# A hybrid RWKV-7, RG-LRU, attention and ConvFFN block on one Trainium2 core: smaller first loads with fifteen constant products, and the output's last row made by token halves

## The chip, the cores and the metric

The kernel runs on one core of one Trainium2 chip. The metric is the device time of one execution in microseconds (us). The kernel before was timed in three runs: 895.38, 891.78 and 893.97 us, median 893.97 us.

## The reference

One layer of a streaming encoder on `x` (1 x 512 tokens x 1024 channels, float32) with a fixed memory `mem` of 256 rows. Every sub-layer begins with an RMS norm. Cut to what matters:

```
h   = rms_norm(x, norm_mix)
p   = h @ W_in + b_in                        # 38 blocks of 128 columns
x  += merge(rwkv7(p[RWKV]), rglru(p[B]))     # two recurrent branches, gated and projected
m   = rms_norm(mem, norm_mem)
k,v = split(m @ W_kv)                        # 1024 columns each
x  += softmax(q k^T / 16) v @ W_o            # q = rms_norm(x) @ W_q, 4 heads
u   = rms_norm(x) @ W_in_ffn                 # 2 x 2816 columns
x  += (gelu(causal_dwconv(u_gate)) * u_up) @ W_out
out = rms_norm(x, norm_fin)
```

Two places are touched by the change: the beginning, where `k` and `v` are made from the memory and `h` from `x`, and the end, where the last product with `W_out` is added to `x`, and the final norm scales the output.

## The kernel before, in words

Everything lies transposed: channels on the 128 partitions, tokens in the columns. A float32 product is made of three products of the type fp32r: each operand is split into a high part (ScalarE rounds it) and a low part (VectorE subtracts the high part from the value), and `mm3` (L165) issues high by high (L166), high by low (L167) and low by high (L168) into one PSUM bank. So each block of 128 weight rows by 128 output rows costs three loads of 128x128 weights and three products over the columns.

Weights are streamed in blocks of 128 x 1024 (512 KB) by SyncE's queue, through four raw buffers, and three buffers each for the high (`wh`) and low (`wl`) part. `stream` (L100) issues the load (L106), the cast on ScalarE (L117) and the remainder on VectorE (L118); the first two blocks are cast in halves of 512 columns. A cast into `wh` waits until TensorE has read the block three back. A scheduler puts the instructions of the program in order on each engine: what stands in `tc.high_priority()` goes as early as it can, `tc.issue_after(x)` puts an instruction behind `x` on its engine, and `keep_in_program_order` keeps the written order.

**The beginning.** TensorE issues `NWAKE` = 11 products of a constant (`wake`, L288), which need no data. The memory `mT` comes in two halves of 512 KB (`load_m`, L296), with the first block of `wk` between them. `split_m(k)` (L304) scales one eighth of the memory by the norm weights `gm` on ScalarE (L306) into the high part and on VectorE (L307) into the low part. Splits 0 to 2 and 3 stand ahead of the casts of the first `wk` block (`fill` with a lambda, L315), the rest behind. Then K is made in eight blocks `m` of 24 products of 256 columns each (`k_ps`), in four banks, two blocks to a bank. The memory's own norm is applied behind the product: squares (`m_squares`, after block 2), their sums `rs_ps` and `rmc_ps` on TensorE (`m_norm`, after block `KNORM` = 5), and then each block is scaled by `rm` into a buffer `kt` (L348, six buffers) and stored to `dK` by GpSimd's queue (L349). V follows: two column halves of 512, for each two banks `v_ps` and 48 products of 512 columns (L166 to L168, with `wv` as the moving side), with the casts of `wv` in the same `wh` and `wl` buffers. `x_norm` (L377) makes `hT`, the normed `x`, in eight parts on VectorE and ScalarE (L382 to L384); the first products with `W_in` (`in_ps`) follow. Small constants for the branches (`dp`, L409 to L452) are made on VectorE after the last block of K.

**The end.** `W_out` is applied in seven groups of products, `out_product` (L1347) for each; the last is `s4`, which adds into the right half of the four banks `YZ` (256 tokens, `oyz_ps`), 4 rows `m` of 11 blocks, 33 products of 256 columns for a row. After each row `c12` (L1422) is called: VectorE adds the bank to `x` (`xr`, L1380), ScalarE squares it (L1382), and for the last row, `m` = 3, this is done for two token halves of 128, and `final` (L1391) follows for each half: the sum of squares over channels on TensorE with a matrix of ones (plain float32, L1394 and L1395), Ln and two Exp on ScalarE (L1406 to L1408), the scaling of all eight channel blocks on GpSimd and VectorE (L1411), and three stores, one by ScalarE's queue (L1415) and two by SyncE's (L1413).

## Time and profile before

| | |
|---|---|
| median of 3 runs | 893.97 us (891.78 to 895.38) |
| profiled execution | 894.56 us, span 892.8 us, mean granted clock 0.996 |
| TensorE busy (PE) | 877.4 us, 98% of the span, 6197 instructions |
| VectorE busy (DVE) | 685.2 us, 77% |
| ScalarE busy (ACT) | 513.6 us, 58% |
| GpSimd busy (POOL) | 132.5 us, 15% |
| DMA | 201.37 MB, mean 226 GB/s |

The profile is of one execution: the span runs from its first to its last recorded event, and all times of rows are in us from its start. PE rows are products, PEld rows are the loads of their weights, which overlap with products. Products are pipelined: a row's own duration (0.28 us for 256 columns) is longer than the distance to the next one, so the price of a product in a stream is the distance from start to start. A row marked "xN" joins N instructions that follow each other on the engine; its duration is from the first to the last. What stands in brackets is the idle time ahead of it and the instruction that ended it. ACTq and SPq rows are issues of DMAs by those engines. The granted clock is TensorE's, as a share of its full 2.4 GHz.

### The profile page before, as it was taken

To read this page: it belongs to the slowest core of one execution; us is meant where nothing else is said; L and a number is where in the kernel's file an instruction comes from. 1 tells how busy PE (TensorE), PEld (TensorE's weight loads), DVE (VectorE), ACT (ScalarE), POOL (GpSimd) and SP (SyncE) were. 2 spreads that over 40 slices of the span, in tenths; PEclk is the share of its full clock that TensorE was granted. 3 is DMA by queue.
4 is the path that set the end of the run, shared out by engine and by line. 5 is a ranking of instruction groups with operands and counts; after the bars stand their busy time and mean duration, and the time that the engine had idled before them with its cause. 6 is when DMAs were issued, how large, how long until landed. Compare 5 with 4: busy or idle time off the path is not lost.

```text
span 892.8 us, 15934 instructions
## 1 busy us (share of the span) xinstructions
PE 877.4 (98%) x6197; PEld 767.9 (86%) x6197; DVE 685.2 (77%) x1104; ACT 513.6 (58%) x783; POOL 132.5 (15%) x163
## 2 busy tenths in 40 slices
PE   8999999999999999999999999999999999999996
PEld 7878878888877677888888778999999999999996
DVE  6796598777967677675575578889888889999674
ACT  6575676634347676233554466766655656757563
POOL 0101222021102021001122111111111111211100
PEclk9999999999999999999999999999999999999999
DMA  7878899678997279758888958999999999998963
GB/s 268 307 253 215 206 228 233 187 203 233 262 227 156 72 203 249 220 166 229 218 234 183 197 137 185 260 275 271 265 255 294 263 297 275 244 276 220 261 202 94
DMA packets 97242, 201.37 MB, mean 226 GB/s; under 512 B 19536, under 2 KB 30928, under 8 KB 97104
## 3 DMA queue, kind: packets, MB, share of 16 engines
q1 hardware_dynamic: 62240, 118.57, 40.4%
q0 software_dynamic: 25504, 67.38, 36.9%
q10 hardware_dynamic: 9424, 14.42, 4.7%
q8 instruction: 48, 0.79, 0.4%
q14 instruction: 26, 0.21, 0.1%
HBM read 188.54 MB, written 78.12 MB: 299 GB/s over the span
## 4 chain that ended last, share of the span: by engine, by line
PE 91%; DVE 4%; DMA 2%; ACT 1%; issue 1%; DVEq 0%; ACTq 0%; SPq 0%
PE in_ps L167 7%; PE in_ps L166 7%; PE in_ps L168 7%; PE fx_ps L167 5%; PE fx_ps L166 5%; PE fx_ps L168 5%; PE fyz_ps L167 4%; PE fyz_ps L166 4%; PE fyz_ps L168 3%; PE ox_ps L166 2%; PE oyz_ps L166 2%; PE ox_ps L168 2%; PE oyz_ps L168 2%; PE oyz_ps L167 2%; PE ox_ps L167 2%; PE co_ps L167 2%
## 5 line engine op out<-in xcount | busy, mean ns | idle before, releaser
L132 ACT CAST wfi_h<-wfi_r 128x1024 fp32r<-128x1024 f32 x77 | 81.1, 1053 | 71.5 <-PE fx_ps L167 19.7
L168 PE MATMUL in_ps<-hT,win_l 128*128 128x512 f32 x304 | 121.3, 399 | 0.0
L167 PE MATMUL in_ps<-hT,win_h 128*128 128x512 f32 x304 | 121.0, 398 | 0.2 <-DVE hT L384 0.2
L166 PE MATMUL in_ps<-hT,win_h 128*128 128x512 f32 x304 | 120.6, 398 | 0.3 <-DVE pr L586 0.3
L133 DVE TENSOR_TENSOR wfi_l<-wfi_r,wfi_h 128x1024 fp32r<-128x1024 f32 x77 | 94.1, 1222 | 22.7 <-ACT wfi_h L132 22.4
L482 POOL DMA_DIRECT2D dS<-in_wfi x66 | 66.7, 1028 | 293.1 <-PE in_ps L166 102.3
L167 PEld LDWEIGHTS in_ps<-hT,win_h 128*128 128x128 f32 x304 | 57.1, 188 | 14.2 <-issue 0.7
L166 PEld LDWEIGHTS in_ps<-hT,win_h 128*128 128x128 f32 x304 | 57.1, 188 | 13.2 <-DVE pr L586 0.7
L168 PEld LDWEIGHTS in_ps<-hT,win_l 128*128 128x128 f32 x304 | 57.1, 188 | 13.1 <-issue 0.7
L518 POOL DMA_DIRECT2D dOs<-in_wfo x54 | 39.8, 784 | 181.5 <-PE fyz_ps L166 54.0
L118 DVE TENSOR_TENSOR win_l<-win_r,win_h 128x1024 fp32r<-128x1024 f32 x38 | 46.3, 1221 | 24.2 <-ACT win_h L117 20.7
L117 ACT CAST win_h<-win_r 128x1024 fp32r<-128x1024 f32 x38 | 39.9, 1050 | 41.1 <-PE in_ps L167 32.4
L1341 DVE TENSOR_TENSOR wfo_l<-wfo_r,wfo_h 128x1024 fp32r<-128x1024 f32 (+1 forms) x39 | 47.2, 1209 | 15.2 <-ACT wfo_h L1340 15.2
L1340 ACT CAST wfo_h<-wfo_r 128x1024 fp32r<-128x1024 f32 (+1 forms) x39 | 40.5, 1039 | 31.3 <-DMA wfo_r<-dOs 11.6
L168 PE MATMUL ox_ps<-go,wfo_l 128*128 128x256 f32 x176 | 49.1, 279 | 0.8 <-DVE wfo_l L1341 0.8
L166 PE MATMUL ox_ps<-go,wfo_h 128*128 128x256 f32 x176 | 49.2, 279 | 0.4 <-ACT wfo_h L1340 0.3
L166 PE MATMUL fx_ps<-hq,wfi_h 128*128 128x256 f32 x176 | 49.4, 280 | 0.0
L166 PE MATMUL fyz_ps<-hq,wfi_h 128*128 128x256 f32 x176 | 49.2, 280 | 0.0
L167 PE MATMUL fx_ps<-hq,wfi_h 128*128 128x256 f32 x176 | 49.2, 280 | 0.0
L167 PE MATMUL fyz_ps<-hq,wfi_h 128*128 128x256 f32 x176 | 49.2, 280 | 0.0
L167 PE MATMUL fx_ps<-hr,wfi_h 128*128 128x256 f32 x176 | 49.2, 280 | 0.0
L166 PE MATMUL fx_ps<-hr,wfi_h 128*128 128x256 f32 x176 | 49.2, 279 | 0.0
(432 smaller groups left out, 2704.9 us busy)
## 6 DMA issues: line engine op xcount, KB each, us to landing
dS<-in_wfi POOLq DMA_DIRECT2D x66, 512.0 KB, 7.8
wfi_r<-dS SPq DMA_DIRECT2D x44, 512.0 KB, 6.8
win_r<-in_win SPq DMA_DIRECT2D x38, 512.0 KB, 5.3
wfi_r<-in_wfi SPq DMA_DIRECT2D x33, 512.0 KB, 5.8
dS<-dS POOLq DMA_DIRECT2D x22, 512.0 KB, 5.7
dOs<-in_wfo POOLq DMA_DIRECT2D x12, 512.0 KB, 7.9
wk_r<-in_wk SPq DMA_DIRECT2D x8, 512.0 KB, 5.1
wv_r<-in_wv SPq DMA_DIRECT2D x8, 512.0 KB, 4.0
```

The lines of the kernel that those rows point to most:

```text
L117: casts.append(S.copy(hi[:, o:o + n], raw[:, o:o + n]))
L118: V.tensor_tensor(lo[:, o:o + n], raw[:, o:o + n], hi[:, o:o + n].bitcast(F32), ALU.subtract)
L132: S.copy(hi, raw)
L133: V.tensor_tensor(lo, raw, hi.bitcast(F32), ALU.subtract)
L166: first = PE.matmul(ps, lh, rh, start=start, stop=False, **kw)
L167: PE.matmul(ps, lh, rl, start=False, stop=False, **kw)
L168: PE.matmul(ps, ll, rh, start=False, stop=stop, **kw)
L482: return lambda: nc.gpsimd.dma_start(s(out), src, **kw)
L518: yield lambda k=k, w=w, src=src: nc.gpsimd.dma_start(dO[n, m][:, k * P:(k + w) * P], src, **kw)
L1340: S.copy(hi[:, :n], raw[:, :n])
L1341: V.tensor_tensor(lo[:, :n], raw[:, :n], hi[:, :n].bitcast(F32), ALU.subtract)
```

## The change

At the beginning: fifteen constant products instead of eleven; the memory's first half comes as two quarters, with the first block of `wk` between them and the second half behind; the splits of the first quarter (two) stand ahead of the first cast and the other six behind it; the squares come after block 1 and the norm after block 4; eight `kt` buffers; and the `dp` operations from the Exp on stand behind the last `hT`. At the end: `out_product` of `s4` makes its last row in two passes of 33 products of 128 columns, one for each token half, keeping the eleven weight blocks; the add and square of the first half are issued after the first pass, its `final` behind the sixth block of the second pass, and the second half's add, square and `final` after that pass.

```diff
--- before.py
+++ after.py
@@ -32,8 +32,8 @@
 IN_REST = [22, 23, 24, 25, 26, 27, 28, 29, 30, 31, 32, 33, 34, 35, 36, 37, 14, 15, 16, 17, 18, 19, 20, 21]
 NEARLY = 3
 NMID = 10
-NWAKE = 11
-KNORM = 5
+NWAKE = 15
+KNORM = 4
 NPOOL = 2
 KVB = 3
 IN_ORDER = IN_RWKV + IN_REST
@@ -293,12 +293,11 @@
         mraw = p0.tile([P, KB, NMEM], F32, name="mraw")
         xraw = p0.tile([P, KB, T], F32, name="xraw")
 
-        def load_m(q):
+        def load_m(k, e):
             with tc.high_priority():
-                mdma.append(tc.keep_in_program_order(
-                    nc.sync.dma_start(mraw[:, 4 * q:4 * q + 4, :], mT_d[:, 4 * q:4 * q + 4, :])))
-
-        load_m(0)
+                mdma.append(tc.keep_in_program_order(nc.sync.dma_start(mraw[:, k:e, :], mT_d[:, k:e, :])))
+
+        load_m(0, 2)
         m2 = p0.tile([P, 2, KB, NMEM], F32R, name="m2")
 
         def split_m(k):
@@ -309,15 +308,15 @@
             return hi
 
         with tc.high_priority():
-            for k in range(3):
+            for k in range(2):
                 split_m(k)
         un = Units(wk_d, "wk")
-        un.fill(lambda i: load_m(1) if i == 0 else split_m(3))
+        un.fill(lambda i: [load_m(2, 4), load_m(4, KB)] if i == 0 else None)
         tc.keep_in_program_order(nc.scalar.dma_start(pv, pv_d))
         mss = p0.tile([P, NMEM], F32, name="mss")
         msq = [p0.tile([P, NMEM], F32, tag="msq", name=f"msq{k}", bufs=2) for k in range(KB)]
         with tc.high_priority():
-            for k in range(4, KB):
+            for k in range(2, KB):
                 last_m = split_m(k)
         def m_squares():
             with tc.issue_after(casts[-1].ins):
@@ -344,7 +343,7 @@
         last_k = None
 
         def k_out(m):
-            kt = p0.tile([P, NMEM], F32, tag="kt", name=f"kt{m}", bufs=6)
+            kt = p0.tile([P, NMEM], F32, tag="kt", name=f"kt{m}", bufs=8)
             ins = V.tensor_tensor(kt, k_ps[m], rm, ALU.mult)
             nc.gpsimd.dma_start(dK[m], kt)
             return ins
@@ -357,7 +356,7 @@
             if m >= 4:
                 with tc.issue_after(wdma[-1].ins):
                     nc.sync.dma_start(xraw[:, 2 * m - 8:2 * m - 6, :], xT_d[:, 2 * m - 8:2 * m - 6, :])
-            if m == 2:
+            if m == 1:
                 m_squares()
             if m == KNORM:
                 m_norm()
@@ -381,7 +380,8 @@
                 hf32 = p0.tile([P, T], F32, tag="hf32", name=f"hf32_{k}", bufs=2)
                 V.scalar_tensor_tensor(hf32, xraw[:, k, :], par("nmix", k), rx, ALU.mult, ALU.mult)
                 S.copy(h2[:, 0, k, :], hf32)
-                V.tensor_tensor(h2[:, 1, k, :], hf32, h2[:, 0, k, :].bitcast(F32), ALU.subtract)
+                last_h = V.tensor_tensor(h2[:, 1, k, :], hf32, h2[:, 0, k, :].bitcast(F32), ALU.subtract)
+            return last_h
 
         st = stream(wv_d, "wv")
         for hf in range(2):
@@ -395,7 +395,7 @@
                         sl = slice(i * P, (i + 1) * P)
                         mm3(pss[i], m2[:, 0, kb, sl], m2[:, 1, kb, sl], rh, rl, kb == 0, kb == KB - 1)
             if hf == 0:
-                x_norm()
+                last_h = x_norm()
             for i in range(2):
                 vt = p0.tile([P, T], F32, tag="vt", name=f"vt{hf}_{i}", bufs=2)
                 S.activation(vt, pss[i], AF.Copy, scale=rmc[:, i:i + 1])
@@ -435,6 +435,7 @@
             V.tensor_scalar(la, lam, -1.0, None, ALU.mult)
             V.tensor_tensor(la, la, lam, ALU.min)
             S.activation(le, la, AF.Exp)
+        with tc.issue_after(last_h.ins):
             V.tensor_scalar(la, le, 2.0, None, ALU.add)
             V.reciprocal(la, la)
             V.tensor_tensor(lz, le, la, ALU.mult)
@@ -1344,9 +1345,9 @@
 
     uf = out_weights()
 
-    def out_product(n, i, out, start, done, nsum=0):
-
-        for m, k in out_order:
+    def out_product(n, i, out, start, done, nsum=0, halves=False):
+
+        for m, k in out_order[:-HB] if halves else out_order:
             wh, wl = next(uf)
             g = gsets[i][k // 8][:, k % 8]
             ins = mm3(out[m], wh, wl, g[:, 0, :], g[:, 1, :], start and k == 0, k == HB - 1,
@@ -1355,6 +1356,19 @@
                 sum_behind(ins)
             if k == HB - 1:
                 done(m)
+        if halves:
+
+            w = [next(uf) for _ in range(HB)]
+            for o in (0, P):
+                for k, (wh, wl) in enumerate(w):
+                    g = gsets[i][k // 8][:, k % 8, :, o:o + P]
+                    ins = mm3(out[MQ - 1][:, o:o + P], wh, wl, g[:, 0, :], g[:, 1, :], False, k == HB - 1,
+                              skip_group_check=True)
+                    if o and k == 5:
+                        with tc.issue_after(ins.ins):
+                            done(MQ - 1, 0, sq)
+                sq = done(MQ - 1, o)
+            done(MQ - 1, P, sq)
 
     def prepare(i, src):
         for k in K4:
@@ -1419,13 +1433,13 @@
         if m == MQ - 1:
             final(cols[0], sq, 2, "x")
 
-    def c12(m):
-        if m < MQ - 1:
-            ffn_out(YZ[m][:, H:T], None, ALU.add, m, cols[1])
-        else:
-            for o in (H, H + P):
-                ts = slice(o, o + P)
-                final(ts, ffn_out(YZ[m][:, ts], None, ALU.add, m, ts, last=True), KB, "yz")
+    def c12(m, o=None, sq=None):
+        if o is None:
+            return ffn_out(YZ[m][:, H:T], None, ALU.add, m, cols[1])
+        ts = slice(H + o, H + o + P)
+        if sq is None:
+            return ffn_out(YZ[m][:, ts], None, ALU.add, m, ts, last=True)
+        final(ts, sq, KB, "yz")
 
     prepare(1, lambda ks: g2(ks, 1))
     prepare(2, lambda ks: g1(ks, 1))
@@ -1449,7 +1463,7 @@
         split_g(0, lambda ks: g1(ks, 1), k)
     out_product("s3", 2, X, False, lambda m: ffn_out(X[m], p5[m], ALU.subtract, MQ + m, cols[1], first=m == 0))
     out_product("A22", 0, X, False, c21)
-    out_product("s4", 1, [t[:, H:T] for t in YZ], False, c12)
+    out_product("s4", 1, [t[:, H:T] for t in YZ], False, c12, halves=True)
 
 
 # ---- launch: one core; inputs and outputs as the reference has them ----
```

On TensorE, V begins elsewhere. Before (names: `k_ps` K's bank, `v_ps` V's banks, `wk_h`, `wv_h` high parts of weights, `m` the split memory), V's products stand behind the two sums and K's seventh block, and the 44 first of them are in one piece:

```order
L168 MATMUL k_ps_284<-m_112,wk_l_319 128x256
L271 MATMUL rs_ps<-mss,ones 128x256 [waits DVE_49]
L338 MATMUL rmc_ps<-ones,mss 128x1 x2
L166 MATMUL k_ps_385<-m_112,wk_h_388 128x256 [waits Activation_49]
L167 MATMUL k_ps_385<-m_112,wk_h_388 128x256
...
L167 MATMUL k_ps_385<-m_112,wk_h_388 128x256
L168 MATMUL k_ps_385<-m_112,wk_l_389 128x256
L166 MATMUL v_ps_0_477<-wv_h_481,m_112 128x512 [waits Activation_49]
L167 MATMUL v_ps_0_477<-wv_l_482,m_112 128x512 [waits DVE_49]
L168 MATMUL v_ps_0_477<-wv_h_481,m_112 128x512
L166 MATMUL v_ps_1_478<-wv_h_481,m_112 128x512 [waits DVE_49]
```

In the change, the sums come a block earlier, K's seventh block stands in the sums' wake, V's first twelve products follow it, and K's sixth block comes behind these twelve:

```order
L271 MATMUL rs_ps<-mss,ones 128x256 [waits DVE_49]
L337 MATMUL rmc_ps<-ones,mss 128x1 x2
L166 MATMUL k_ps_390<-m_116,wk_h_393 128x256 [waits Activation_49]
L167 MATMUL k_ps_390<-m_116,wk_h_393 128x256
...
L168 MATMUL k_ps_390<-m_116,wk_l_394 128x256
L166 MATMUL v_ps_0_482<-wv_h_486,m_116 128x512 [waits Activation_49]
L166 MATMUL v_ps_1_483<-wv_h_486,m_116 128x512 [waits DVE_49]
L167 MATMUL v_ps_0_482<-wv_l_487,m_116 128x512 [waits DVE_49]
...
L167 MATMUL v_ps_1_483<-wv_l_487,m_116 128x512
L168 MATMUL v_ps_1_483<-wv_h_486,m_116 128x512
L166 MATMUL k_ps_289<-m_116,wk_h_358 128x256 [waits DVE_49]
L167 MATMUL k_ps_289<-m_116,wk_h_358 128x256
```

What moved: V's first product went ahead of K's sixth block, and its waits for ScalarE's cast and VectorE's remainder with it.

On ScalarE the beginning (names: `m` the high part of the memory, `gm` the norm weights, `wk_h` the first cast block) before:

```order
L306 ACTIVATE m_112<-mraw,gm 128x256 [waits DMAHW1_49,DMAHW0_49]
L306 ACTIVATE m_112<-mraw,gm 128x256 x3
L117 CAST wk_h_122<-wk_r_119 128x512 [waits DMAHW2_49]
L117 CAST wk_h_122<-wk_r_119 128x512
L316 DMA pv<-in_pv 128x240
L306 ACTIVATE m_112<-mraw,gm 128x256 [waits DMAHW3_49]
L306 ACTIVATE m_112<-mraw,gm 128x256 x3
```

and in the change:

```order
L305 ACTIVATE m_116<-mraw,gm 128x256 [waits DMAHW1_49,DMAHW0_49]
L305 ACTIVATE m_116<-mraw,gm 128x256
L117 CAST wk_h_125<-wk_r_121 128x512 [waits DMAHW2_49]
L117 CAST wk_h_125<-wk_r_121 128x512
L305 ACTIVATE m_116<-mraw,gm 128x256 [waits DMAHW3_49]
L305 ACTIVATE m_116<-mraw,gm 128x256
...
L305 ACTIVATE m_116<-mraw,gm 128x256 [waits DMAHW4_49]
L305 ACTIVATE m_116<-mraw,gm 128x256 x3
```

What moved: two splits stand ahead of the first cast now, four before.

At the end of TensorE's program (`oyz_ps` the bank, `go` the gated input, `wfo_h` and `wfo_l` the weights, `rs_ps` the sums) before:

```order
L166 MATMUL oyz_ps_8128<-go_3_8115,wfo_h_9480 128x256
L167 MATMUL oyz_ps_8128<-go_3_8115,wfo_h_9480 128x256
L168 MATMUL oyz_ps_8128<-go_3_8115,wfo_l_9481 128x256
L1394 MATMUL rs_ps_9500<-sso,ones 128x128 [waits DVE_49]
L1394 MATMUL rs_ps_9517<-sso,ones 128x128
L1395 MATMUL rs_ps_9500<-t_3_256_9497,ones 128x128 [waits Activation_49]
L1395 MATMUL rs_ps_9517<-t_3_384_9514,ones 128x128 [waits Activation_49]
```

and in the change, from the end of the first token half on, with a piece of the second half around its first sum:

```order
L167 MATMUL oyz_ps_8133<-go_3_8120,wfo_h_9464 128x128
L168 MATMUL oyz_ps_8133<-go_3_8120,wfo_l_9465 128x128
L166 MATMUL oyz_ps_8133<-go_8_8119,wfo_h_9450 128x128 [waits DVE_49]
L167 MATMUL oyz_ps_8133<-go_8_8119,wfo_h_9450 128x128
...
L167 MATMUL oyz_ps_8133<-go_8_8119,wfo_h_9450 128x128
L168 MATMUL oyz_ps_8133<-go_8_8119,wfo_l_9451 128x128
L1408 MATMUL rs_ps_9523<-sso,ones 128x128
L1409 MATMUL rs_ps_9523<-t_3_256_9502,ones 128x128 [waits Activation_49]
L166 MATMUL oyz_ps_8133<-go_8_8119,wfo_h_9450 128x128
L167 MATMUL oyz_ps_8133<-go_8_8119,wfo_h_9450 128x128
```

What moved: the second half's first product waits for VectorE (its add of the first half out of the same bank), and the first half's two sums stand among the second half's products.

## Rows read from the trace of the kernel before

**Rows 1.** The chain of waits that ended last, whole span, shares by engine

```profile
PE 91%; DVE 4%; DMA 2%; ACT 1%; issue 1%; DVEq 0%; ACTq 0%; SPq 0%
```

**Rows 2.** TensorE's waits, whole span: us in total, times, longest

```profile
PE k_ps L166 <- ACT wk_h L117: 2.3, 1, 2.3
...
PE k_ps L166 <- DVE kt L348: 0.8, 1, 0.8
```

**Rows 3.** Timeline of the beginning: start, us, engine, line, what [idle before <-releaser]

```profile
4.48 1.29 PE L288 MATMUL wake<-onesr 128*128 128x512 f32 x4
...
5.80 1.30 ACT L306 ACTIVATE m<-mraw,gm 128x256 fp32r<-128x256 f32 x3 [3.31 <-DMA gm<-in_pv]
6.34 1.68 DVE L307 SCALAR_TENSOR_TENSOR m<-mraw,gm,m 128x256 fp32r<-128x256 f32 x4 [5.03 <-ACT m L306]
...
7.41 1.12 ACT L117 CAST wk_h<-wk_r 128x512 fp32r<-128x512 f32 x2
8.05 1.29 DVE L118 TENSOR_TENSOR wk_l<-wk_r,wk_h 128x512 fp32r<-128x512 f32 x2
...
8.07 0.39 PE L166 MATMUL k_ps<-m,wk_h 128*128 128x256 f32 x1 [2.29 <-ACT wk_h L117]
```

**Rows 4.** Windows of the beginning: us, busy PE, PEld, DVE, ACT, POOL, PEclk, DMA share, GB/s

```profile
5.78:8.07 2.29, 0.00 (x1) 0.01 (x1) 1.71 (x5) 2.27 (x6) 0.00 (x0) 1.00 1.02 415
...
8.32:11.73 3.41, 3.29 (x15) 2.98 (x15) 3.41 (x8) 3.41 (x8) 0.00 (x0) 0.50 1.04 415
```

**Rows 5.** Timeline around V's first products

```profile
27.05 1.05 ACT L117 CAST wv_h<-wv_r 128x1024 fp32r<-128x1024 f32 x1
...
28.13 1.23 DVE L118 TENSOR_TENSOR wv_l<-wv_r,wv_h 128x1024 fp32r<-128x1024 f32 x1 [0.39 <-ACT wv_h L117]
...
30.64 0.39 PE L166 MATMUL v_ps<-wv_h,m 128*128 128x512 f32 x1
...
30.87 0.39 PE L167 MATMUL v_ps<-wv_l,m 128*128 128x512 f32 x1
```

**Rows 6.** Timeline around K's last block

```profile
41.40 0.42 DVE L348 TENSOR_TENSOR kt<-k_ps,rm 128x256 f32<-128x256 f32 x1 [1.59 <-DMA dK<-kt]
...
41.88 0.38 PE L166 MATMUL k_ps<-m,wk_h 128*128 128x256 f32 x1 [0.81 <-DVE kt L348]
```

**Rows 7.** Timeline around the last part of `hT`

```profile
64.88 0.16 DVE L440 TENSOR_TENSOR dp<-dp 128x4 f32<-128x4 f32 x1
...
67.15 0.50 PE L167 MATMUL in_ps<-hT,win_h 128*128 128x512 f32 x1 [0.24 <-DVE hT L384]
```

**Rows 8.** Timeline of TensorE in the last group, ten products apart

```profile
879.08 0.28 PE L166 MATMUL oyz_ps<-go,wfo_h 128*128 128x256 f32 x1
...
880.26 0.28 PE L167 MATMUL oyz_ps<-go,wfo_h 128*128 128x256 f32 x1
```

**Rows 9.** Timeline of weight loads of eight one-column sums (PEld)

```profile
439.01 0.97 PEld L1062 LDWEIGHTS rxc_ps<-ones,ssx 128*128 128x128 f32 x8 [0.26 <-issue]
439.89 0.19 PEld L167 LDWEIGHTS q_ps<-hx,wq_h 128*128 128x128 f32 x1
```

**Rows 10.** Timeline of the end

```profile
883.56 0.28 PE L168 MATMUL oyz_ps<-go,wfo_l 128*128 128x256 f32 x1
...
883.67 0.61 PE L1394 MATMUL rs_ps<-sso,ones 128*128 128x128 f32 x4
883.87 0.49 DVE L1380 TENSOR_TENSOR xr<-xr,oyz_ps 128x128 f32<-128x128 f32 x2 [2.56 <-PE oyz_ps L168]
...
885.91 1.95 DVE L1411 TENSOR_TENSOR xr<-xr,ro_ps 128x384 f32<-128x384 f32 x4 [0.89 <-ACT ro_ps L1407]
...
886.50 1.31 ACTq L1415 DMA_DIRECT2D out<-xr  x2
887.19 2.26 SPq L1413 DMA_DIRECT2D out<-xr  x4
```

**Rows 11.** Stores issued by L1413, from issue to landing

```profile
L1413 SPq DMA_DIRECT2D out<-xr x4: 373/459/691, 887.2 to 888.8; - x4
...
DMA to landing us min/median/max: 1.9/2.8/2.8
```

## The prediction

> **What bounds the kernel now.** I read the chain of waits first: nine tenths of it is TensorE [rows 1], so a term counts only where TensorE waits or gets other work, and after its last product, where nothing covers the tail. TensorE's own waits come next: two of the four largest touch the change [rows 2], 2.3 us for the first cast weight and 0.8 us for a `kt`. Then I read three stretches of the timeline around such waits, and the last 10 us. The reference is the profiled execution, 894.56 us with a span of 892.8 us, 0.6 us above the median of 893.97; I apply the sum of differences to the median. About 0.5% (4.5 us) is what a measurement of this kernel can tell from no change.
>
> **The beginning.** ScalarE starts at 5.80 us because the small `gm` lands then, not the memory [rows 3], so a smaller first transfer brings the first split no earlier. What the new order brings is that two splits instead of four stand ahead of the first cast. Four took until 7.41, about 0.41 each; after the change the cast starts at 5.80 + 2 × 0.41 = 6.62. The first product started 0.66 after the cast; so it will start at about 7.25 instead of 8.07: 0.8 us. The DMA queues are full there, 415 GB/s [rows 4], and the first cast followed its splits without idle; its transfer, now behind 256 KB less, comes 0.6 us earlier and does not hold it.
>
> The clock matters more. TensorE is idle for 2.29 us ahead of its first product [rows 3], and the granted clock is 0.50 from 8.32 to 11.73 (1.2 GHz, the lower of its two levels); 15 products fall there [rows 4], seven more at 0.118 follow, and the second block starts at about 12.7. Four more constants (four now end at 5.77 [rows 3]; one at full clock takes what V's products of the same width take, 0.23 [rows 5]) run until 6.7, ahead of 7.25: they delay nothing and leave some 0.5 us of idle. If the clock then stays at 1.00, VectorE bounds the first block: from 7.25 two remainders of a half weight (1.29 [rows 3]) and six splits (1.68 for four [rows 3], so 2.5) end at 11.0, the last products at 11.2: 1.5 us earlier. If it is low from 8.32 to 11.73 all the same, three more products are done before and the wait of 0.4 for the first remainder falls ahead of it: 0.6 us. No end lies below that, as no added constant ends after the first product could start. I take 1.5, since most of the idle ahead of the fall goes, and keep 0.6.
>
> The sums of squares come a block earlier, and twelve of V's products are put ahead of K's sixth block. With eight `kt` buffers VectorE's `kt` no longer waits for the store of another (1.59 us), and TensorE's stall of 0.81, with the 0.17 by which its products otherwise overlap, goes [rows 6]: 1.0 us (0.7 if part of it comes back at another `kt`). But V now begins right behind a K block, and the cast of V's first weights waits until that block's second-last product has freed one of three `wh` buffers. Before, that cast stood at 27.05 and its remainder at 28.13, both under the 24 products that ran until V began at 30.64 [rows 5]; now nothing covers them. TensorE waits for the cast (1.05 us and 0.08 of start) and, after the two products that need the high part alone, for the remainder (1.23 less two products of 0.23): 1.13 + 0.8 = **1.9 us lost**. The bounds are 1.1, if the remainder is hidden, and 2.3, if neither product covers it.
>
> Small `dp` operations stand ahead of the last `hT` on VectorE from 64.88, and at 67.15 TensorE has lost 0.24 of idle, 0.16 of overlap and 0.1 by a longer first product: 0.5 [rows 7]. They go behind it. VectorE works through that stage without a break, so I count half of the 0.5 as back: 0.25 (0 to 0.5). GpSimd's order and SyncE's outside the beginning stay as they are.
>
> Beginning together: 1.5 + 1.0 − 1.9 + 0.25 = **0.85 us gained**, between 0.6 + 0.7 − 2.3 + 0 = 1.0 lost and 1.5 + 1.0 − 1.1 + 0.5 = 1.9 gained.
>
> **The end.** The last output row's 33 products of 256 columns, 0.118 us apart [rows 8], become 66 of 128 columns. Each of the 66 still loads 128×128 weights. No product of this number type with under 256 columns is in the trace, so its price has to be bounded. From below: by columns alone it is a line through 0.118 for 256 and V's 0.23 for 512 [rows 5, 8], 0.06. From above: a plain fp32 sum of 128 columns takes two of four rows 0.11 apart (0.61 us for the four, the last 0.27 long) [rows 10], 0.22. Between them stands the nearest row: eight products of one column, whose loads are 0.110 apart with nothing else to set their pace [rows 9]. So a load of this size sets a floor there, and I take 0.114, between it and the 256-column price. Then 66 × 0.114 = 7.5 against 33 × 0.118 = 3.9: +3.6. At the ends, 66 × 0.06 and 66 × 0.22: +0.1 and +10.6.
>
> The Trainium skill, "TensorE: Matmul & The Clock Gate", section "Back-to-back issue gap", gives a sustained spacing of about 81 ns for products of 128 columns and 131 ns for 512; the second figure is not what this trace shows (0.23 us for V's [rows 5]), and by the first, as an estimate, this term would be 66 × 0.081 − 3.9 = +1.4 and the end +0.4 in place of the +2.6 below.
>
> Two waits are new on TensorE. The second half writes the bank from which VectorE still adds the first half, so its first product waits for that add, and every later product waits behind it. The add starts 0.31 after the last product's start and takes 0.25 [rows 10]; with 0.08 until TensorE starts, less the spacing of 0.11 that it has anyway: 0.53. And the first half's sum, four plain rows of 0.11, stands behind 18 of the second half's products, when its square has long been done: 0.44. The logarithm, exponentials, multiplies and 512 KB of stores of the first half run beside the second half's 33 products (3.8 us) and so cost nothing; on ScalarE the store of the first half, which waits for VectorE's multiply, stands ahead of the second half's square, and if that cover is gone (at 0.06 a product, 2 us for the 33) it holds that square by up to 0.5.
>
> Behind the last product one half's tail remains. Now it goes: add 883.87, multiplies 885.91, stores issued from 886.50 to 889.4, the last of them at 888.8, landing 2.8 us later, 891.6 [rows 10, 11]. With one half there are two multiplies in place of four on VectorE and three stores in place of six, the last issued at about 887.4 and landing in 2.1 (of the landings' 1.9 to 2.8, a shorter one, as the queues hold half): 889.5, **2.0 us saved** (1.4 to 2.4).
>
> End: 3.6 + 0.53 + 0.44 − 2.0 = **+2.6 us**. With 0.06 it is 0.1 + 1.0 − 2.0 + 0.5 = −0.4; with 0.22, 10.6 + 1.0 − 2.0 = +9.6.
>
> **Sum:** 893.97 − 0.85 + 2.6 = **895.7 us**.
>
> **The rivals.**
> *Columns set the price, not the load.* For it: 512 columns cost twice what 256 do [rows 5, 8], so columns set the pace there. Against it: the one-column loads [rows 9]. The end is −0.4 and the time 893.97 − 0.85 − 0.4 = 892.7. Chance 0.19.
>
> *Half columns go at the plain rate (the other side, slower by far).* If a product of under 256 columns is worked through like the plain sums, the last row takes 66 × 0.22 on TensorE, with nothing beside it, and the time is 893.97 − 0.85 + 9.6 = 902.7. From 0.087 us a product on, the whole change loses, and from 0.155 on it loses over 4.5 us. For it: the only 128-column products at the end go so [rows 10]. Against: they are of another number type. Chance 0.14.
>
> *The beginning gives nothing.* The clock falls again, or V's wait is longer because its weights land late. Then the beginning is between 0 and 1.0 lost and the time 893.97 + 2.6 to 893.97 + 3.6, about 897. For it: the same fall in this trace [rows 4]. Chance 0.10.
>
> *Everything falls out well.* V's cast is hidden after all, columns set the price and the tail saves its 2.4: 893.97 − 2.75 − 0.8 = 890.4. Against it: three buffers and the order of the casts, which nothing changes. Chance 0.05; my forecast has 0.52 and a range of its own of 893.5 to 898.
>
> **How the numbers follow.** The predicted time is the likeliest case's. The range takes in that case, the cheap columns, the lost beginning with its bounds and 1 to 2 us for the spread of the runs: 890.8 to 899.5; the plain rate and half of the favourable case are left out. Slower by over 0.5% (above 898.4) are the plain rate and a sliver of the lost beginning, 0.16; faster by over 0.5% (below 889.5) the favourable case with luck in the runs and some of the cheap columns, 0.07; the rest, 0.77, is within it.
>
> **What would show it.** In the profile after: products of 128 columns 0.11 us apart in the last row (0.06 or 0.22 by the rivals); an idle of some 0.5 us ahead of its second half, ended by the add into `xr`; a granted clock of 1.00 from 8 to 12 us; about 1.1 and 0.8 us of idle ahead of V's first products, ended by the cast and the remainder; no wait for `kt`; the end of the span about 7 us after the last product instead of 9. I am wrong if the last row takes under 6 or over 9 us, or if V's first products follow K without idle.

## The result, and the profile after

| | before | after |
|---|---|---|
| median of 14 runs each | 893.75 us (890.05 to 896.48) | 896.88 us (894.19 to 899.0) |
| profiled execution | 894.56 us, span 892.8 | 897.73 us, span 896.0 |
| TensorE busy | 877.4 us, 6197 instructions | 882.3 us, 6234 instructions |

The ratio is 1.0034 with a 95% interval of 1.0024 to 1.0045: 3.0 us slower (2.1 to 4.0), where 1.7 us slower was forecast (895.7, range 890.8 to 899.5). It lies within the 0.5% of no change, on the forecast side. The same program, timed once more in the experiments, gave 1.0022 (1.0009 to 1.0035).

The beginning after the change, from the timeline (columns as in [rows 3]), and below it the windows (as in [rows 4]):

```profile
4.71 0.91 ACT L305 ACTIVATE m<-mraw,gm 128x256 fp32r<-128x256 f32 x2 [2.25 <-DMA gm<-in_pv]
4.74 1.78 PE L288 MATMUL wake<-onesr 128*128 128x512 f32 x7
...
5.78 1.14 ACT L117 CAST wk_h<-wk_r 128x512 fp32r<-128x512 f32 x2 [0.15 <-DMA wk_r<-in_wk]
...
6.45 0.39 PE L166 MATMUL k_ps<-m,wk_h 128*128 128x256 f32 x1
```

```profile
8.32:11.73 3.41, 3.41 (x27) 3.28 (x28) 3.33 (x8) 3.41 (x9) 0.00 (x0) 1.00 1.04 417
```

The first split (of the memory into high and low part) starts 1.1 us earlier than in [rows 3], the first product 1.6 us earlier and with no idle behind the constants. The stretch that held 15 products at a granted clock of 0.50 [rows 4] now holds 27 at 1.00. The second block starts 2.1 us earlier (10.66 against 12.80).

Then V. The timeline of its first products, and the windows around them:

```profile
25.79 1.04 ACT L117 CAST wv_h<-wv_r 128x1024 fp32r<-128x1024 f32 x1 [0.65 <-PE k_ps L167]
...
26.89 0.73 PE L166 MATMUL v_ps<-wv_h,m 128*128 128x512 f32 x2 [1.02 <-ACT wv_h L117]
26.94 1.22 DVE L118 TENSOR_TENSOR wv_l<-wv_r,wv_h 128x1024 fp32r<-128x1024 f32 x1
...
28.21 0.64 PE L167 MATMUL v_ps<-wv_l,m 128*128 128x512 f32 x1 [0.59 <-DVE wv_l L118]
...
29.07 0.63 PE L167 MATMUL v_ps<-wv_l,m 128*128 128x512 f32 x1
...
29.50 0.63 PE L168 MATMUL v_ps<-wv_h,m 128*128 128x512 f32 x1
```

```profile
26.50:28.41 1.91, 0.93 (x3) 0.50 (x4) 1.88 (x5) 0.69 (x2) 0.00 (x0) 1.00 1.01 384
28.41:31.83 3.42, 3.42 (x9) 2.65 (x9) 3.04 (x11) 0.80 (x2) 2.90 (x5) 0.50 0.94 304
31.83:35.20 3.37, 3.37 (x28) 3.29 (x27) 1.73 (x2) 2.21 (x4) 0.00 (x0) 1.00 0.86 321
```

The cast was held until K's block freed its buffer ("<-PE k_ps"), and TensorE waited for the cast and then for the remainder, as forecast. What was not forecast is the second window: after these two idles the granted clock is 0.50 for 3.42 us, and V's products stand 0.43 us apart instead of 0.23 [rows 5].

The end, last row, with the first loads of weights (PEld):

```profile
880.47 0.22 PE L166 MATMUL oyz_ps<-go,wfo_h 128*128 128x128 f32 x1
880.47 0.19 PEld L167 LDWEIGHTS oyz_ps<-go,wfo_h 128*128 128x128 f32 x1
880.53 0.28 PE L167 MATMUL oyz_ps<-go,wfo_h 128*128 128x128 f32 x1
880.58 0.19 PEld L168 LDWEIGHTS oyz_ps<-go,wfo_l 128*128 128x128 f32 x1
880.64 0.27 PE L168 MATMUL oyz_ps<-go,wfo_l 128*128 128x128 f32 x1
...
883.99 0.27 PE L168 MATMUL oyz_ps<-go,wfo_l 128*128 128x128 f32 x1
884.64 0.33 PE L166 MATMUL oyz_ps<-go,wfo_h 128*128 128x128 f32 x1 [0.38 <-DVE xr L1394]
...
886.59 0.28 PE L168 MATMUL oyz_ps<-go,wfo_l 128*128 128x128 f32 x1
886.71 0.43 PE L1408 MATMUL rs_ps<-sso,ones 128*128 128x128 f32 x2
886.98 0.39 PE L1409 MATMUL rs_ps<-t,ones 128*128 128x128 f32 x2
887.12 0.31 PE L166 MATMUL oyz_ps<-go,wfo_h 128*128 128x128 f32 x1
...
888.72 0.27 PE L168 MATMUL oyz_ps<-go,wfo_l 128*128 128x128 f32 x1
```

From 880.64 to 883.99 lie thirty spacings: 0.112 us each for half the columns. The products could go faster: the row's first is followed by the next after 0.06 us, once, while the loads keep standing 0.11 apart (880.47, 880.58). The second half starts 0.65 after the first half's last product (0.54 more than a spacing), and the sums take 887.12 − 886.59 − 0.11 = 0.42. The row's first product starts at 880.47 and its last at 888.72, 8.25 us against 3.77 before; behind the last product's start 7.23 us remain against 9.23. Together 15.48 against 13.00. (The 256-column products ahead of the row stand 0.113 us apart in this execution and 0.118 in the profile before.)

TensorE's waits after the change:

```profile
PE fyz_ps L166 <- ACT p L1270: 1.5, 1, 1.5
...
PE v_ps L166 <- ACT wv_h L117: 1.0, 1, 1.0
PE fx_ps L166 <- ACT sn L1275: 0.6, 1, 0.6
PE v_ps L167 <- DVE wv_l L118: 0.6, 1, 0.6
```

The waits for `kt` and for the first cast [rows 2] are gone. Two in the middle (`fx_ps` at 607 us, `fyz_ps` at 725 us) are new, though the instructions there are the same and in the same order; e5 below tells whether they belong to the program. Where the two programs reach the same product: at 76 us the change is 0.2 us ahead, at 800 us it is 1.8 behind, at the last row 0.7 behind (the kernel before has a wait of 0.8 for a weight's remainder in the last groups that this execution has not).

### The profile page after: what moved, and what is told of

It reads as the page before. It is cut to its first block, busy times and chain, and to the rows that moved or that the text cites. A ratio compares the mean times of both kernels' runs of the same rounds, so it can differ in the third digit from the quotient of the medians.

```text
span 896.0 us, 16007 instructions
## 1 busy us (share of the span) xinstructions
PE 882.3 (98%) x6234; PEld 773.2 (86%) x6234; DVE 685.0 (76%) x1104; ACT 514.4 (57%) x783; POOL 132.5 (15%) x163
## 4 chain that ended last, share of the span: by engine, by line
PE 90%; DVE 4%; DMA 3%; ACT 1%; issue 1%; POOLq 0%; POOL 0%; SPq 0%; ACTq 0%; DVEq 0%
PE in_ps L166 8%; PE in_ps L167 8%; PE in_ps L168 8%; PE fx_ps L166 4%; PE fx_ps L168 4%; PE fx_ps L167 4%; PE fyz_ps L166 3%; PE fyz_ps L168 3%; PE fyz_ps L167 3%; PE ox_ps L166 2%; PE ox_ps L168 2%; PE ox_ps L167 2%; PE oyz_ps L166 2%; PE oyz_ps L168 2%; PE oyz_ps L167 2%; PE co_ps L167 2%
## 5 line engine op out<-in xcount | busy, mean ns | idle before, releaser
L167 PEld LDWEIGHTS in_ps<-hT,win_h 128*128 128x128 f32 x304 | 57.1, 188 | 13.5 <-issue 0.7
L1342 DVE TENSOR_TENSOR wfo_l<-wfo_r,wfo_h 128x1024 fp32r<-128x1024 f32 (+1 forms) x39 | 47.0, 1206 | 12.6 <-ACT wfo_h L1341 12.6
L166 PE MATMUL fyz_ps<-hq,wfi_h 128*128 128x256 f32 x176 | 49.3, 280 | 1.5 <-ACT p L1270 1.5
L166 PE MATMUL fx_ps<-hr,wfi_h 128*128 128x256 f32 x176 | 49.3, 280 | 0.6 <-ACT sn L1275 0.6
L168 PE MATMUL fx_ps<-hq,wfi_l 128*128 128x256 f32 x176 | 49.3, 280 | 0.0
L168 PE MATMUL fyz_ps<-hq,wfi_l 128*128 128x256 f32 x176 | 49.3, 280 | 0.0
L168 PE MATMUL fx_ps<-hr,wfi_l 128*128 128x256 f32 x176 | 49.2, 280 | 0.0
```

What stands on the lines that cost most here:

```text
L166: first = PE.matmul(ps, lh, rh, start=start, stop=False, **kw)
L167: PE.matmul(ps, lh, rl, start=False, stop=False, **kw)
L168: PE.matmul(ps, ll, rh, start=False, stop=stop, **kw)
L1342: V.tensor_tensor(lo[:, :n], raw[:, :n], hi[:, :n].bitcast(F32), ALU.subtract)
```

## The experiments

Each run's ratio is to the kernel before, timed on the same chip; e7, e8 and e9 are single runs without a ratio. Three marks in us are read from each timeline: when the second block of K starts, when the 101st product with `W_in` starts (by then the whole beginning is paid for), and how long the end takes, from the last row's first product to the end of the span.

| run | ratio (95%) | 2nd block | 101st `W_in` product | end |
|---|---|---|---|---|
| before | | 12.80 | 81.00 | 13.00 |
| after | 1.0034 (1.0024 to 1.0045) | 10.66 | 80.82 | 15.48 |
| e1 end alone | 1.0019 (1.0003 to 1.0034) | 13.51 | 81.85 | 15.55 |
| e2 beginning alone | 0.9990 (0.9975 to 1.0005) | 11.01 | 81.17 | 12.95 |
| e3 e2, norm after block 5 | 0.9976 (0.9963 to 0.9989) | 10.88 | 79.11 | 12.95 |
| e4 e2, V's first cast in its own buffer | 0.9991 (0.9976 to 1.0007) | 10.97 | 80.95 | 12.97 |
| e5 after again | 1.0022 (1.0009 to 1.0035) | 10.54 | 80.70 | 15.49 |
| e6 after, norm after block 5 | 1.0015 (1.0003 to 1.0027) | 10.80 | 79.41 | 15.47 |
| e7, e12 (e3 with 11 constants) | e7 one run, 890.24 us; e12 0.9979 (0.9964 to 0.9994) | 10.90, 10.66 | 78.53, 79.27 | 12.83, 12.97 |
| e8, e11 (before with 8 `kt` buffers) | e8 one run, 889.86 us; e11 0.9983 (0.9969 to 0.9996) | 10.95, 12.61 | 79.45, 79.32 | 13.01, 13.01 |
| e9 e6 in 192 and 64 columns | one run, 895.52 us | 10.74 | 78.97 | 16.46 |
| e10 e6, halves for 3 of 11 blocks | 1.0000 (0.9987 to 1.0013) | 10.46 | 78.94 | 13.83 |

**e1 and e2, each part alone.** e1 is the kernel before with the new `out_product` and `c12`; e2 is the change with the old ones.

```diff
-    out_product("s4", 1, [t[:, H:T] for t in YZ], False, c12)
+    out_product("s4", 1, [t[:, H:T] for t in YZ], False, c12, halves=True)
```

> The kernel before with the last row by token halves and nothing else changed. My theory (the end costs what the trace after shows: 66 products at 0.112 us instead of 33 at 0.113, a wait of 0.53 for the add, 0.42 for the first half's sum, 2.0 less behind the last product): 2.4 us slower than the kernel before, 896.2. Rival one (the end costs nothing, and what the change lost lies in the weight and DMA waits of the middle, which differ between the two profiled executions by about 1 us): within 0.7 us of the kernel before.

> The change without the token halves: the beginning alone. My theory (TensorE gains 2.1 us up to its second block, 1.0 at K's last block, and gives both back where V waits 1.6 us for its first cast and remainder and then makes nine products at 0.427 instead of 0.233 us): within 0.5 us of the kernel before. Rival one (the forecast: the clock stays up at V): 0.85 us faster, 892.9. Rival two (the earlier beginning moves later loads into worse waits): 0.7 us slower or more.

e1 is 1.7 us slower by its ratio (0.3 to 3.0), and its trace gives 2.55 us more for the end; the rival of a free end falls. e2 is 0.9 us faster by its ratio (2.2 faster to 0.4 slower), which takes in the forecast's 0.85 and no change alike; its trace shows why the gain is small. The waits of V and the low clock are there as in the change, and the 101st `W_in` product is at 81.17, as late as before. The forecast's number holds within the interval, its cause (the clock staying up at V) does not.

**e3, V in its old place.** Only the block behind which the memory's norm stands.

```diff
-KNORM = 4
+KNORM = 5
```

> The beginning alone, with the memory's norm after block 5 again (KNORM 5), by which the scheduler puts V behind K's sixth and seventh block as before. My theory: no wait at V's first product, no low clock there, the gain of the first blocks and of the kt buffers stays: 2 to 3 us faster, about 891.2. Rival (the gain is taken by the next wait, TensorE for the parts of hT, which VectorE makes without a break): within 0.7 us of the kernel before.

2.1 us faster (1.0 to 3.3). The sums go back behind K's sixth block, the scheduler puts V's 44 products in one piece again, and the cast is covered: 

```profile
27.05 1.04 ACT L117 CAST wv_h<-wv_r 128x1024 fp32r<-128x1024 f32 x1
...
28.77 0.39 PE L166 MATMUL v_ps<-wv_h,m 128*128 128x512 f32 x1
...
29.40 0.50 PE L167 MATMUL v_ps<-wv_l,m 128*128 128x512 f32 x1 [0.24 <-DVE wv_l L118]
...
32.94 0.50 PE L167 MATMUL v_ps<-wv_l,m 128*128 128x512 f32 x1 [0.48 <-DVE wv_l L118]
```

```profile
28.41:31.83 3.42, 3.18 (x16) 2.43 (x15) 3.32 (x7) 2.83 (x8) 0.00 (x0) 1.00 0.64 223
```

The same 3.42 us hold 16 products at a clock of 1.00, not 9 at 0.50. Against e2 the beginning is 2.06 us shorter (79.11 against 81.17). So one constant of the program, `KNORM`, cost the change its beginning. V now waits for two remainders instead, 0.7 us together.

**e4, the buffer.** V's first block gets a high and a low buffer from another pool.

```diff
-                hi = wp.tile([P, 1024], F32R, tag="wh", name=f"{name}_h{g}")
-                lo = wp.tile([P, 1024], F32R, tag="wl", name=f"{name}_l{g}")
+                if own is not None and g == 0:
+                    hi = own.tile([P, 1024], F32R, name=f"{name}_h{g}")
+                    lo = own.tile([P, 1024], F32R, name=f"{name}_l{g}")
...
-        st = stream(wv_d, "wv")
+        st = stream(wv_d, "wv", own=p0)
```

> The beginning alone with the order of the change (norm after block 4), but V's first weight block cast into a buffer of its own, so that its cast no longer waits for a block of K. My theory (the buffer is what V waits for): no idle ahead of V's first products, granted clock 1.00 there, 2 to 3 us faster than the kernel before. Rival (the weights of V land too late in any case, or the cast delays K's last cast by its 1.05 us): an idle of 1 us stays somewhere before V, and the time is within 0.7 us of the kernel before.

The half of the theory on the buffer held: V's first product follows K's last without idle, and the clock stays at 1.00.

```profile
25.86 0.28 PE L172 MATMUL k_ps<-m,wk_l 128*128 128x256 f32 x1
...
25.98 0.39 PE L170 MATMUL v_ps<-wv_h,m 128*128 128x512 f32 x1
```

The time did not follow: 0.8 us faster (2.1 faster to 0.6 slower), and the beginning ends where it ended before (80.95). The buffer is not all that differs: with it the scheduler puts 22 of V's products ahead of K's next block, not 12. TensorE's waits between 20 and 80 us:

```profile
PE v_ps L171 <- DVE wv_l L122: 0.8, 1, 0.8
PE rs_ps L167 <- DVE rx_l L165: 0.5, 1, 0.5
PE k_ps L170 <- DVE kt L351: 0.5, 1, 0.5
PE v_ps L170 <- DVE rmt L265: 0.3, 1, 0.3
```

All four are waits for VectorE, which has the norms and V's remainders to make in the same stretch when V begins early. The wait moved; it did not go. The time came out nearer the rival's, by another way than the rival said: no idle stayed ahead of V.

**e5 and e6, do the parts add up?** e5 is the change, e6 the change with `KNORM = 5`.

> The change itself, beside the next kernels. My theory (beginning and end add up): the sum of the two parts timed alone, 0.9990 and 1.0019, so a ratio near 1.001 (895), and no wait above 1 us between 80 and 860 us that the kernel before has not. Rival one (the parts do not add up, the earlier or later middle of this program meets its weights worse): a ratio of 1.003 or more, with the waits of the first profile (fx_ps for a ScalarE operation behind a cast, 0.6 and 1.5 us) back in their places.

> The change with the memory's norm after block 5 (KNORM 5), the token halves kept. My theory: the beginning's 2.1 us (ratio 0.9976 alone) and the end's 1.7 to 2.4 us cancel: within 0.8 us of the kernel before. Rival (the parts do not add up): 1.5 us or more slower.

e5's ratio, 1.0022, lies between the two numbers. The parts' sum is 0.9990 + 0.0019 = 1.0009, with some 0.0015 of uncertainty on either part; the change's two timings lie above it, 1.0022 within that and 1.0034 at its edge. So the sum is not excluded, and not confirmed. e5's trace decides more: between 80 and 860 us it has neither of the two new waits of the first profile, and it reaches 829 us 0.6 us ahead of the kernel before instead of 1.8 behind. The two waits belonged to one execution (the first lies behind a weight whose DMA took 10.8 us), not to the program. e6 is 1.3 us slower (0.3 to 2.4), neither of what was expected: 0.8 was my bound and 1.5 the rival's, both in the interval. Its trace has both parts as they are alone, 79.41 and 15.47. Its ratio too lies above its parts' sum (0.9976 + 0.0019 = 0.9995). All three sums would fit better if the end costs the 2.5 us that every trace of it shows, and not the 1.7 of e1's ratio; that is an inference from the traces.

**e7 and e12, the constants; e8 and e11, the buffers.**

```diff
-NWAKE = 15
+NWAKE = 11
```

> The beginning alone with KNORM 5 and eleven constants. Theory one (the constants decide the clock of the first block): idle of over 1 us between the constants and the first product, granted clock 0.50 over a stretch between 7 and 12 us, the second block starts about 1 us later than with fifteen (12.2 instead of 11.2 us). Theory two (the earlier first product does it alone): clock 1.00 from 5 us on, second block at 11.2.

> The beginning alone with KNORM 5 and eleven constants, timed. Theory one (with the first product at 6.4 us the constants no longer decide the clock, as one look showed): the same as with fifteen, a ratio of 0.9976 within 0.001. Theory two (without the four the clock falls in part of the executions): 1 us slower than with fifteen, a ratio near 0.999 and the clock of the first 14 us low in its profile.

```diff
-            kt = p0.tile([P, NMEM], F32, tag="kt", name=f"kt{m}", bufs=6)
+            kt = p0.tile([P, NMEM], F32, tag="kt", name=f"kt{m}", bufs=8)
```

> The kernel before with eight kt buffers and nothing else. My theory (the sixth kt waited for a buffer's store, and TensorE for that kt): no wait of TensorE for kt at 41 to 42 us, V's last bank about 1.0 us earlier against K's sixth block. Rival (VectorE's kt is late for the norm itself): the wait stays above 0.5 us.

> The kernel before with eight kt buffers, timed. My theory (its one look, 889.86 us, was in part luck of the clock in the first block): 1.0 us faster than the kernel before, the stall it takes away, a ratio near 0.999. Rival (the eight buffers are worth all that the beginning with KNORM 5 brings, and the loads and constants nothing): a ratio of 0.9976 or less.

Eleven constants give what fifteen give (0.9979 against 0.9976), the second block at 10.90 and 10.66, the clock at 1.00 behind the constants in both profiles: theory two of e7 and theory one of e12. In e7 the first product at 6.43 follows constants that end at 6.39; the four more have nothing to fill. They can be in the way: in e4, e9 and e10 the constants kept the slow pace longer, the fifteen ended at 7.4 to 7.7, and K's first product stood right behind them, 0.5 to 0.9 us later than its cast allowed (0.66 after the cast's start [rows 3]). e9 has

```profile
1.33 6.40 PE L288 MATMUL wake<-onesr 128*128 128x512 f32 x15 [1.33 <-DVE Pp L617]
7.57 0.28 PE L166 MATMUL k_ps<-m,wk_h 128*128 128x256 f32 x1
```

behind a cast that started at 6.03. It cost nothing that the marks show: their second blocks start at 10.46 to 10.97, as the others' do.

The eight buffers alone take the wait for `kt` away; the product that started at 41.88 [rows 6] follows its neighbour at a normal spacing in e8's timeline:

```profile
40.19 0.40 PE L167 MATMUL v_ps<-wv_l,m 128*128 128x512 f32 x1
40.42 0.28 PE L166 MATMUL k_ps<-m,wk_h 128*128 128x256 f32 x1
```

They are worth 1.5 us by the ratio (0.4 to 2.8), between theory and rival, and not to be told from e3's 2.1. The pair e8 and e11 shows more: one program, two executions (on two chips), and the first block's clock differs:

```profile
8.32:11.73 3.41, 3.41 (x29) 3.41 (x30) 3.35 (x8) 3.41 (x8) 0.00 (x0) 1.00 1.03 406
```

```profile
9.46:12.87 3.41, 3.41 (x19) 3.41 (x18) 3.38 (x6) 3.41 (x9) 0.00 (x0) 0.50 0.90 351
```

(e8 above, e11 below.) The second block starts 1.7 us apart, V 1.3 us (28.79 and 30.06), and the 101st `W_in` product at 79.45 and 79.32: the whole gain of the first block is gone by then. In e8 V waits 0.8 us for remainders, in e11 not at all. The other runs agree: of the ten that keep V behind K's seventh block, the seven whose second block starts by 11.0 us wait 0.5 to 1.4 us for V's remainders, and the three where it starts at 12.6 to 13.5 (before, e1, e11) do not. The loads and constants of the change therefore bring the first block forward, and V gives most of it back. The six runs with e3's beginning (e3, e6, e7, e9, e10, e12) reach the 101st product at 78.53 to 79.41, 0.3 us ahead of e8 and e11 on average; e8 and e11 still wait 0.3 and 0.4 us for `hT`, which the six do not, so that move of `dp` alone may account for it. That V is held by its weights' arrival, cast and remainder in a row is how I read it; it wasn't tried by loading them earlier.

**e9 and e10, what a piece costs.** e9 splits the last row at 192 columns, e10 splits only its last three weight blocks (both on e6).

```diff
-            for o in (0, P):
+            for o, e in ((0, 192), (192, H)):
...
-                    g = gsets[i][k // 8][:, k % 8, :, o:o + P]
+                    g = gsets[i][k // 8][:, k % 8, :, o:e]
...
```

```diff
+            for k in range(8):
+                g = gsets[i][0][:, k]
+                mm3(out[MQ - 1], *w[k], g[:, 0, :], g[:, 1, :], False, False, skip_group_check=True)
             for o in (0, P):
                 for k, (wh, wl) in enumerate(w):
+                    if k < 8:
+                        continue
...
-                    if o and k == 5:
+                    if o and k == HB - 1:
```

> The change with KNORM 5, and the last row in pieces of 192 and 64 columns in place of 128 and 128. Theory one (the load of 128x128 weights sets the pace of every product under 256 columns): 192 and 64 columns both 0.112 us apart, the last row as long as in the change, and the end of the span some 0.7 us nearer to the last product, as the last piece's tail is half as wide. Theory two (columns and a fixed part set it, 0.112 at 128 by chance): 64 columns under 0.09 and 192 columns above 0.112.

> The beginning with KNORM 5, and only the last three of the last row's eleven weight blocks made by token halves, so that 9 products are added in place of 33. My theory (every added product costs 0.112, the wait for the add 0.5, and the first half leads by 1.6 us only, so that VectorE's multiplies end about 1 us nearer to the last product than before): 0.5 us slower than the beginning with KNORM 5 alone, a ratio near 0.998 to the kernel before. Rival (it is the split tail that costs, not the added loads): the ratio of the whole halves with KNORM 5, 1.0015.

e9's timeline, a piece of each width, and then one late in the 64 columns, with the windows of the last two:

```profile
878.05 0.27 PE L167 MATMUL oyz_ps<-go,wfo_h 128*128 128x192 f32 x1
878.16 0.28 PE L168 MATMUL oyz_ps<-go,wfo_l 128*128 128x192 f32 x1
...
882.03 0.28 PE L167 MATMUL oyz_ps<-go,wfo_h 128*128 128x64 f32 x1
882.14 0.28 PE L168 MATMUL oyz_ps<-go,wfo_l 128*128 128x64 f32 x1
...
885.18 0.40 PE L168 MATMUL oyz_ps<-go,wfo_l 128*128 128x64 f32 x1
885.39 0.40 PE L166 MATMUL oyz_ps<-go,wfo_h 128*128 128x64 f32 x1
```

```profile
881.56:884.10 2.54, 2.54 (x21) 2.54 (x22) 0.32 (x1) 0.34 (x1) 0.00 (x0) 1.00 0.03 6
884.40:887.10 2.70, 2.70 (x16) 2.70 (x14) 1.42 (x2) 1.12 (x3) 0.99 (x1) 0.50 0.01 2
```

At a clock of 1.00 products of 64, 128 and 192 columns all stand 0.11 us apart: the load sets the pace, as theory one has it. The rest of its forecast missed: the clock fell to 0.50 within the 64-column products, each then took 0.21, and the row grew to 9.8 us; the tail shrank by 0.6 where 0.7 was expected.

e10 times as the kernel before (1.0000, 0.9987 to 1.0013), between theory and rival. Its end takes 13.83, 0.83 more than the unsplit one where 0.5 was expected: the row is 1.5 longer, as costed (9 × 0.112 and 0.54), but the tail only 0.67 shorter instead of 1. A smaller split loses less; none of the three sizes gained.

## Why the prediction was right, and where it was not

**The end** was right term by term in the trace: +4.48 for the row (3.6 + 0.53 + 0.44 = 4.57 forecast), 2.0 less behind it (2.0 forecast), together +2.48 against +2.6, and the same within 0.1 in every trace with whole halves (15.47 to 15.55). The choice of 0.114 by the one-column loads [rows 9] carried it; the products took 0.112. The Trainium skill, "TensorE: Matmul & The Clock Gate", section "LDWEIGHTS (loading the stationary operand)", has a load take its columns divided by 1.2 GHz; for 128 columns that is, as an estimate, 107 ns. The products at a granted clock of 1.00 agree (112 ns); those of e9 at 0.50 stand 214 ns apart and do not. The 81 ns that the Trainium skill gives on the same page, section "Back-to-back issue gap", is not what these products show either.

**The beginning** was forecast at 0.85 us gained. It came out at 0.2 by the trace of the change (81.00 against 80.82), at 0.3 by e5's and at 0.2 lost by e2's, and at 0.9 gained by e2's ratio, with an interval that takes in all of these. So the agreement of that ratio with the forecast is luck: two of its terms were wrong, and against each other. Term by term:

| step | forecast | in the trace after |
|---|---|---|
| second block earlier | 1.5 | 2.1 |
| `kt` wait gone | 1.0 | 1.0 |
| V waits for cast and remainder | −1.9 | −2.0 (three late starts: 1.18, 0.10, 0.75) |
| clock at V | 0 | −1.6 (eight spacings of 0.43 for 0.23) |
| wait for the last `hT` gone | 0.25 | 0.5 |
| sum | 0.85 | 0.0 (0.2 by the marks) |

Two steps failed. "A smaller first transfer brings the first split no earlier" was wrong: `gm` comes in by its own queue, but it came earlier with the smaller transfer beside it. From issue to landing it took 5.0 us before and 3.9 after; in all ten runs with quarters 3.5 to 4.1, in the four with halves 4.5 to 5.0. In 13 of these 14 runs it landed 0.16 to 0.18 us behind the memory's first piece. That the piece sets its pace is how I read it; no run changed the piece alone. Before, and below it after:

```profile
L291 ACTq DMA_DIRECT2D gm<-in_pv x1: 427/427/427, 0.7 to 0.7; - x1
...
DMA to landing us min/median/max: 5.0/5.0/5.0
```

```profile
L291 ACTq DMA_DIRECT2D gm<-in_pv x1: 407/407/407, 0.7 to 0.7; - x1
...
DMA to landing us min/median/max: 3.9/3.9/3.9
```

And the 1.9 us at V were costed at a full clock. The forecast had the same mechanism in hand for the first block (idle ahead, clock 0.50 behind [rows 4]) and left it out at the one place where it added new idle; all three executions with these idles (after, e2, e5) have the low clock there, and e3 and e4, without them, do not. The two errors, +0.6 and −1.6, and half of the `hT` wait underestimated, leave the sum 0.85 too good, and that, with runs that spread by 5 us, is most of the distance from 895.7 to 896.88. The rival "the beginning gives nothing" was nearest: 897, by the clock, but at V and not in K's first block. A smaller step was wrong without cost: added constants were to "delay nothing", and in e4, e9 and e10 they held the first product back.

The term of 1.5 us for the first block's clock was also no fixed difference. Of the four executions with the memory in halves three had that block at the low pace (before, e11, and e1 with 16 products in the same 3.41 us, its clock's record beginning later) and e8 not; of the ten with quarters none. The idle ahead of the first product was 1.1 us in e8 and 1.5 to 2.3 in those three. The Trainium skill, "TensorE: Matmul & The Clock Gate", section "What's actually happening", says that the number of slow products at a kernel's start differs from run to run of one kernel. The pair e8 and e11 agrees: 0.50 in the first block of one, 1.00 in the other's. And a gain there is mostly returned at V, as e8 and e11 show, which the forecast did not follow up.

## What to carry to other kernels

Here, halving a product's columns from 256 halved nothing, as every product loads its own 128×128 weights: price a split by the load (0.11 us here), and set it against what the shorter tail saves. Where a change puts a wait on TensorE, cost the stretch behind it too: two idles of 1.0 and 0.6 us were followed by 3.4 us at half the clock. Ask what waits next for a stage that is made faster: here V returned what K's first block gained. And time the parts alone: here the eight buffers alone (1.5 us faster than before) and the new beginning with `KNORM` 5 and no token halves (2.1 us faster) both beat the two kernels, and the whole hid it.

## What the runs showed of the hardware

In one execution the granted clock fell while TensorE was busy: in e9 it went to 0.50 at 884.40 us, after an idle of 0.45 and 2.8 us of 64-column products 0.112 us apart with the first piece's sums among them, and stayed there to the row's end. In the change the second half's 128-column products, at the same pace behind an idle of 0.38, ran at 1.00 from 884.64 to the row's end. Whether the columns make the difference isn't shown: e9 is one execution. The spacing that the load sets doubled with the fall, from 0.112 to 0.214 us.
